# First feed-forward rows read before the last scan, later ones a tile at a time, and the sample's rows three blocks later

## The chip, the cores and the metric

The kernel runs on one core of a Trainium2 chip. The metric is the device time of one execution in microseconds (us). The engines are TensorE (PE in the profile; PEld is its weight load), VectorE (DVE), ScalarE (ACT), GpSimd (POOL) and SyncE (SP, which only issues DMAs here). Each engine works through its own queue in order; semaphores tie the queues together.

## What is computed

One layer of a streaming encoder, for a prompt of 2048 rows and a sample of 32 rows that continues from caches, all in float32 with 1024 channels:

```python
xn = rms_norm(x, norm_mix_g);  proj = xn @ w_in              # 1024 -> 2176 columns
y_a = conv_module(u_a)       # GLU, causal depthwise conv of width 31, layer norm, swish
y_b = rwkv7_mixer(u_b)       # delta-rule state update, 4 heads of 64: a scan over the rows
y_c = pool_mixer(u_c)        # trailing means over 2, 4, 8, 16 rows
y_d = window_attention(u_d)  # 4 query heads, 2 kv heads, window 128
x = x + concat(y_a, y_b, y_c, y_d) @ w_out
hn = rms_norm(x, norm_ffn_g)
x = x + (silu(hn @ w_gate) * (hn @ w_up)) @ w_down           # inner width 2816
```

The outputs are both streams' rows and the new states and caches.

## The kernel before

**Matrix products.** A float32 factor is split into a high part and a remainder (`fp32r`), and each product is three matmuls (lines 93 to 95 in helper `mm3`).

**Mixer stage.** The prompt goes through in `NB` = 8 blocks of 256 rows. For each block a string of letters gives the order in which its steps are issued: A is the projection of the other mixers, R the scan, n and N the norm of the next block's rows, B and S the next block's projection and the preparation of its scan, O the output projection of the block before, P and D the attention's preparation and the attention itself, L the pooling, C the convolution, Y the end of the scan's mixer. The last block has a string of its own, `ORDS`. Within the program, Tile's scheduler then sets each engine's order by issue order and by priorities (`high_priority(offset=...)`; R and Y have 1000). The attention of a block is two row tiles of 128, one after the other on single buffers: transposes `atp`, scores `asp`, softmax in `apr` on VectorE and ScalarE, transposes `aptp`, product `aot`, result `yhd` and `yld`.

**The sample.** Its 32 rows ride along with one block, `SB`: the block's projections are 288 rather than 256 columns wide, and its P, C and L follow there. R and O of the sample come one block later. `SB` is 1, the second block. Blocks one and two also read the raw weights and split them on ScalarE and on GpSimd or VectorE (`wraw`, `whl`); later blocks reload split copies from memory (`wk_i`, `wk_o`).

**Feed-forward, first half.** The 2080 rows are taken in three blocks `FB` of 704, 704 and 672 rows. For each, `ffn_x` reads six row tiles of `x2d`, norms them (`xs`, L1220) and transposes them into `xT` (TensorE `xps` L1224, evacuated by VectorE at L1226). It then forms the sums of a seven-product (Strassen-like) scheme in `ft` (L1234 to L1237). `ffn_ops` splits the seven operands into `xh` (ScalarE, L1251) and `xl` (VectorE, L1252). Then 11 pairs of column tiles follow; each pair is two halves, gate and up, of seven products of 12 matmuls `gu`. In a half VectorE also forms sums of weights (`wf`, L1265 to L1268) and evacuates `u` and `act` (L1299 to L1334), ScalarE makes `wh` and GpSimd `wl` (L1274, L1275).

```python
1212         for c in range(0, n, 128):                       # ffn_x, six row tiles
1219             rsqrt(st[:m, 1:2], st[:m, 0:1], 1.0 / D, RMS_EPS)
1220             V.tensor_scalar(xs[:m], xs[:m], st[:m, 1:2], None, op0=MUL)
...
1344     with tc.high_priority(offset=1500):
1345         xT = ffn_x(*FB[0], bank0)                        # behind the eighth block's steps
1346     xo = ffn_ops(xT, FB[0][1] // 2)
1347     out_proj(*pend)                                      # output projection of block eight
...
1358         for g in range(NP):
1359             if g == NP - 2 and i + 1 < len(FB):          # all six tiles of the next block
1360                 with tc.high_priority(offset=FNP):
1361                     xT = ffn_x(*FB[i + 1], ...)
1362             ffn_pair(r0, n, g, xo, H)
```

So before, the first block's rows are read and transposed after the last scan is issued, and a later block's six tiles and its sums are issued in one go late in the block ahead of it.

**Feed-forward, second half.** The inner activations go through memory (`act_d`) and are multiplied by the split down weights (`dn`, L1372 to L1408).

**Buffers.** The mixers' SBUF pools `b1`, `b2`, `b4` and `bv` lie on one side and are released together (`p0.close()`); the pool `fx` with `xT`, `xs` and `ft` is opened after that. `xT`, `ft` and each operand have one buffer.

Of the kernel before, what the change touches and what calls it, by code (L numbers as in the profile page):

```python
# [32 lines left out]
def layer(tc, ins, outs):  # L33
# [14 lines left out]
    SB = 1 if NB > 1 else 0  # L48
# [20 lines left out]
    ORDS = "ARnNBSOPLCYD,ARPDCLOY".split(",")  # L69
# [8 lines left out]
    SEP = 0  # L78
# [76 lines left out]
    b4 = p0.enter_context(tc.tile_pool(name="b4", bufs=1, side="right"))  # L155
    bv = p0.enter_context(tc.tile_pool(name="bv", bufs=1, side="right"))
# [12 lines left out]

    gmix = cp.tile([128, D], F32, tag="gm", name="gmix")  # L170
# [234 lines left out]
    def rs(sg, res):  # L405
        return res_s if sg is seg_s else res["p"]
# [4 lines left out]
    def sgs(b, o):  # L411
        return [sg for sg in (seg_p, seg_s) if at_block(sg, b, o)]
# [672 lines left out]
    def mix_y(outs_, ys):  # L1085
        for sg, o in outs_:
            rwkv_out(sg, *o, *yy(sg, ys)["b"])
# [63 lines left out]
    with tc.high_priority(offset=100000):  # L1151
        xhl = norm(0, norm_load(0))
    with tc.high_priority(offset=PB0):
        res = proj_b(0, *xhl)
        for sg in sgs(0, "R") if SEP else [seg_p]:
            rwkv_prep(sg, rs(sg, res))
    pend = None
    for b in range(NB):
        ys = y_tiles()
        cur = res  # L1160
        for o in ORDS[max(b - NB, -len(ORDS))]:
          with tc.high_priority(offset=OFF[o]) if o in OFF else ExitStack():
            if o == "R":
                ro = mix_b(b, cur, ys)
            if o == "Y":
                mix_y(ro, ys)
            if o == "O" and pend is not None:
                out_proj(*pend)
            if o == "A":
                proj(b, cur, *xhl)  # L1170
            if o == "P":
                mix_p(b, cur)
            if o == "D":
                mix_d(b, cur, ys)
            if o == "C":
                mix_a(b, cur, ys)
            if o == "L":
                mix_c(b, cur, ys)
            if o == "n" and b + 1 < NB:
                xn = norm_load(b + 1)  # L1180
            if o == "N" and b + 1 < NB:
                xhl = norm(b + 1, xn)
            if o == "B" and b + 1 < NB:
                res = proj_b(b + 1, *xhl)
            if o == "S" and b + 1 < NB:
                for sg in sgs(b + 1, "R") if SEP else [seg_p]:
                    rwkv_prep(sg, rs(sg, res))
        pend = (b, ys)
    p0.close()

# [13 lines left out]
    fx = pool2("x", "right", px2)  # L1204
    fo = pool2("o", "right")
# [3 lines left out]
    def ffn_x(r0, n, bank):  # L1209

        xT = fx.tile([128, 2 * NF * 128], F32, tag="xT", name="xT")[:, :KT * 2 * HM].rearrange("p (k t) -> p k t", k=KT)
        for c in range(0, n, 128):
            m = min(128, n - c)
            xs = fx.tile([128, D], F32, tag="xs", name="xs", bufs=XSB)
            st = fx.tile([128, 4], F32, tag="xst", name="xst", bufs=2)
            junk = fx.tile([128, D], BF16, tag="fjunk", name="fjunk")
            nc.sync.dma_start(xs[:m], x2d[r0 + c:r0 + c + m])
            S.activation(junk[:m], xs[:m], AF.Square, accum_out=st[:m, 0:1])
            rsqrt(st[:m, 1:2], st[:m, 0:1], 1.0 / D, RMS_EPS)
            V.tensor_scalar(xs[:m], xs[:m], st[:m, 1:2], None, op0=MUL)  # L1220
            for g in range(0, KT, 4):
                ps = bank()
                for j in range(4):
                    TE.transpose(ps[:, j, :m], xs[:m, (g + j) * 128:(g + j + 1) * 128], ident[:m, :m])  # L1224
                with tc.high_priority(offset=EVP):
                    V.tensor_tensor(xT[:, g:g + 4, c:c + m], ps[:, :, :m],  # L1226
                                    gcol[:, g:g + 4].unsqueeze(2).to_broadcast([128, 4, m]), op=MUL)
# [152 lines left out]
    for hf in range(D // 512):  # L1380
# [3 lines left out]
        for t in range(TT // 128 + 1):  # L1384
            n = min(128, TT - t * 128)
            e = t % 2
            af = d2.tile([128, NF, 128], F32, tag="af", name="af") if e else fx.tile(
# [9 lines left out]
            xr = d2.tile([128, 512], F32, tag="xr", name="xr", bufs=2)  # L1397
# [52 lines left out]
```

## Time and profile before

| | |
|---|---|
| median of 3 runs (range) | 2536.8 us (2535.28 to 2550.27) |
| profiled execution, and its span | 2535.49 us, 2533.8 us |
| mean granted TensorE clock | 0.975 |
| PE, DVE, ACT, POOL busy | 2401.4, 1729.2, 982.2, 977.3 us |
| instructions | 44039 |

The span runs from the first to the last instruction on the core. Busy time of PE is the union of overlapping matmuls, so it hides lost issue slots; the number of matmul records in a stretch tells more. A row "us, PE busy (x)" of the table of stretches gives its length, each engine's busy time and in brackets its instructions, then the granted clock and the DMA share. In the timeline a row is start, duration, engine, line, output<-input, and in square brackets how long the engine had waited and for whom.

### The profile page before, as it was taken

What the parts mean: (1) busy time and instruction counts of PE and PEld (TensorE: products, weight loads), DVE (VectorE), ACT (ScalarE), POOL (GpSimd) and SP (SyncE); (2) the same over time, 40 slices, a digit from 0 to 9 for tenths busy, and PEclk for the clock granted to TensorE, in tenths of its full rate; (3) what the DMA queues carried; (4) which work ended last, traced back from release to release, by engine and by line L of the source; (5) the groups of instructions that cost most, each with busy time, mean ns of one, the idle gap of its engine ahead of it and who ended that gap; (6) DMA issues with size and microseconds to landing.
All of it is one profiled execution on the core that took longest, in us unless ns stands there. A gap on an engine that the chain in (4) does not pass through costs nothing. (4 is left out here: it accounts for less than half of the span.)

```text
span 2533.8 us, 44039 instructions
## 1 busy us (share of the span) xinstructions
PE 2401.4 (95%) x16433; PEld 2196.0 (87%) x16433; DVE 1729.2 (68%) x3697; ACT 982.2 (39%) x2138; POOL 977.3 (39%) x834
## 2 busy tenths in 40 slices
PE   7789899999999999789999999998999899999999
PEld 6778788888988988689999999998999878878887
DVE  6798969896969698686877868678777432233221
ACT  5445453534353434434445443454444331122110
POOL 5543521211111112377677776676777310001000
PEclk9899899999999999899999999999999899999999
DMA  6556558566767676633433333334333465445441
GB/s 204 192 208 241 204 205 319 206 226 229 277 256 272 228 266 226 239 93 104 130 103 106 102 103 108 103 98 133 112 103 116 126 198 139 133 122 166 135 137 34
DMA packets 350747, 424.69 MB, mean 168 GB/s; under 512 B 24530, under 2 KB 300259, under 8 KB 326979
## 3 DMA queue, kind: packets, MB, share of 16 engines
q1 hardware_dynamic: 325304, 380.76, 46.4%
q10 hardware_dynamic: 25227, 41.10, 4.3%
q8 instruction: 129, 2.11, 0.3%
q14 instruction: 87, 0.71, 0.1%
HBM read 354.72 MB, written 67.18 MB: 167 GB/s over the span
## 5 line engine op out<-in xcount | busy, mean ns | idle before, releaser
L1275 POOL TENSOR_TENSOR wl<-wf,wh 128x512 fp32r<-128x512 f32 x462 | 661.8, 1438 | 241.0 <-PE gu L95 192.7
L93 PE MATMUL gu<-xh,wh 128*128 128x352 f32 (+1 forms) x1848 | 591.4, 324 | 25.8 <-DVE u L1302 19.2
L95 PE MATMUL gu<-xh,wl 128*128 128x352 f32 (+1 forms) x1848 | 598.6, 324 | 4.1 <-POOL wl L1275 4.1
L94 PE MATMUL gu<-xl,wh 128*128 128x352 f32 (+1 forms) x1848 | 597.6, 324 | 3.3 <-DVE xl L1252 3.2
L1274 ACT ACTIVATE wh<-wf 128x512 fp32r<-128x512 f32 x462 | 288.2, 630 | 434.2 <-PE gu L94 305.1
L93 PEld LDWEIGHTS gu<-xh,wh 128*128 128x128 f32 x1848 | 350.3, 190 | 31.1 <-DVE u L1302 19.0
L94 PEld LDWEIGHTS gu<-xl,wh 128*128 128x128 f32 x1848 | 351.6, 190 | 5.4 <-DVE xl L1252 5.4
L95 PEld LDWEIGHTS gu<-xh,wl 128*128 128x128 f32 x1848 | 351.0, 190 | 5.4 <-POOL wl L1275 5.3
L93 PE MATMUL dn<-dw,ah 128*128 128x512 f32 x704 | 277.4, 396 | 9.1 <-ACT dw L1376 6.7
L94 PE MATMUL dn<-dw,ah 128*128 128x512 f32 x704 | 276.0, 393 | 2.0 <-DVE dw L1377 1.9
L95 PE MATMUL dn<-dw,ah 128*128 128x512 f32 x704 | 275.6, 392 | 1.0 <-DVE ah L1396 1.0
L93 PE MATMUL pj<-xh,whl 128*128 128x256 f32 (+1 forms) x832 | 249.1, 302 | 11.8 <-ACT gb_s L526 3.1
L94 PE MATMUL pj<-xl,whl 128*128 128x256 f32 (+1 forms) x832 | 245.4, 297 | 0.7 <-DVE xl L144 0.6
L95 PE MATMUL pj<-xh,whl 128*128 128x256 f32 (+1 forms) x832 | 242.2, 295 | 3.9 <-POOL whl L387 3.9
L1395 ACT ACTIVATE ah<-af 128x1408 fp32r<-128x1408 f32 (+1 forms) x68 | 86.5, 1321 | 369.5 <-issue 291.8
L1408 DVE TENSOR_TENSOR xr<-xr,dn 128x512 f32<-128x512 f32 x32 | 22.0, 687 | 303.2 <-PE dn L95 303.2
L568 DVE SCALAR_TENSOR_TENSOR accp<-gbp,d_cws,accp 128x256 f32<-128x256 f32 x480 | 227.3, 501 | 0.8
L93 PEld LDWEIGHTS pj<-xh,whl 128*128 128x128 f32 x832 | 164.3, 198 | 23.5 <-issue 6.9
L95 PEld LDWEIGHTS pj<-xh,whl 128*128 128x128 f32 x832 | 162.0, 196 | 7.7 <-POOL whl L387 5.7
L94 PEld LDWEIGHTS pj<-xl,whl 128*128 128x128 f32 x832 | 164.0, 198 | 3.8 <-DVE xl L144 1.6
L93 PEld LDWEIGHTS dn<-dw,ah 128*128 128x128 f32 x704 | 133.0, 189 | 39.3 <-ACT dw L1376 7.4
L94 PEld LDWEIGHTS dn<-dw,ah 128*128 128x128 f32 x704 | 133.0, 189 | 31.5 <-DVE dw L1377 2.8
(512 smaller groups left out, 4764.0 us busy)
## 6 DMA issues: line engine op xcount, KB each, us to landing
whl<-wk_i SPq DMA_DIRECT2D x104, 1024.0 KB
whl<-wk_o SPq DMA_DIRECT2D x56, 1024.0 KB
af<-act_d SPq DMA_DIRECT2D x32, 1408.0 KB
wf<-in_ffn_w_gate_dram SPq DMA_DIRECT2D x132, 256.0 KB
wf<-in_ffn_w_up_dram SPq DMA_DIRECT2D x132, 256.0 KB
wk_i<-whl SPq DMA_DIRECT2D x16, 1024.0 KB
act_d<-act ACTq DMA_DIRECT2D x44, 352.0 KB
wraw<-in_w_in_dram SPq DMA_DIRECT2D x96, 128.0 KB
```

The lines of the kernel that those rows point to most:

```text
L93: TE.matmul(out, ah, bh, start=first, stop=False, skip_group_check=more)
L94: TE.matmul(out, ah, bl, start=False, stop=False, skip_group_check=more)
L95: TE.matmul(out, al, bh, start=False, stop=last, skip_group_check=more)
L568: V.scalar_tensor_tensor(acc[:, c, :], gb[:, c, j:j + T], cws[c][:, j:j + 1], acc[:, c, :], op0=MUL, op1=ADD)
L1274: S.activation(hi, q[nm], AF.Copy)
L1275: G.tensor_tensor(lo, q[nm], hi.bitcast(F32), op=SUB)
L1395: S.activation(ah[:, fs_, :n], af[:, fs_, :n], AF.Copy)
L1408: V.tensor_tensor(xr, xr, ps, op=ADD)
```

## The change

Four edits, in one diff:

- 14 products of the identity with itself, into a PSUM tile that nobody reads, first in TensorE's queue.
- `SB` is 4: the sample's rows go with the fifth block, its R and O with the sixth.
- `ffn_x` becomes a generator that yields after each row tile, and the sums become a function of their own, `ffn_sums`. A new letter X in the last block's string, behind P and ahead of R, runs `ffn_x` for the first block. D now stands behind R there. For that, `b1` is released alone at X, the other mixer pools lie on the other side, and PSUM for `xps` comes from the buffers `at` and `nx` rather than `at` and `rk`.
- Later blocks: one row tile in each of the pairs g = 2 to 7, the sums at g = 8.

```diff
-    SB = 1 if NB > 1 else 0
+    SB = 4 if NB > 5 else 0
-    ORDS = "ARnNBSOPLCYD,ARPDCLOY".split(",")
+    ORDS = "ARnNBSOPLCYD,APXRDCLOY".split(",")
-    p0 = ExitStack()
+    p0, pb = ExitStack(), ExitStack()
-    b1 = p0.enter_context(tc.tile_pool(name="b1", bufs=1, side="right"))
-    b2 = p0.enter_context(tc.tile_pool(name="b2", bufs=2, side="right"))
+    b1 = pb.enter_context(tc.tile_pool(name="b1", bufs=1, side="right"))
+    b2 = p0.enter_context(tc.tile_pool(name="b2", bufs=2, side="left"))
...
+    with tc.high_priority(offset=200000):
+        warm = px([128, 128], "warm", "rk")
+        for _ in range(14):
+            TE.matmul(warm, ident, ident, start=True, stop=True)
...
     def ffn_x(r0, n, bank):
...
+            yield xT
+
+    def ffn_sums(xT, n):
+
         H = n // 2
         q = {"b11": xT[:, 0:4, 0:H], ...}
-        ft = fx.tile([128, 3, 4, HM], F32, tag="ft", name="ft")
+        ft = fq.tile([128, 3, 4, HM], F32, tag="ft", name="ft")
...
-        return px([128, 4, 128], "xps", ("at", "rk")[banks[0] % 2])
-
-    with tc.high_priority(offset=1500):
-        xT = ffn_x(*FB[0], bank0)
-    xo = ffn_ops(xT, FB[0][1] // 2)
+        return px([128, 4, 128], "xps", ("at", "nx")[banks[0] % 2])
...
+            if o == "X":
+                pb.close()
+                fx = pool2("x", "right", px2)
+                for xT in ffn_x(*FB[0], bank0):
+                    pass
...
+    fq, fo = pool2("q", "right", px2), pool2("o", "right")
+    xo = ffn_ops(ffn_sums(xT, FB[0][1]), FB[0][1] // 2)
     out_proj(*pend)
...
         if i:
             with tc.high_priority(offset=FNP):
-                xo = ffn_ops(xT, H)
+                xo = ffn_ops(q, H)
         for g in range(NP):
-            if g == NP - 2 and i + 1 < len(FB):
+            if g == NP - 9 and i + 1 < len(FB):
+                rows = ffn_x(*FB[i + 1], lambda: pnr.tile([128, 4, 128], F32, tag="nr", name="xps"))
+            if g >= NP - 9 and i + 1 < len(FB):
                 with tc.high_priority(offset=FNP):
-                    xT = ffn_x(*FB[i + 1], lambda: pnr.tile([128, 4, 128], F32, tag="nr", name="xps"))
+                    xT = next(rows, xT)
+                    if g == NP - 3:
+                        q = ffn_sums(xT, FB[i + 1][1])
             ffn_pair(r0, n, g, xo, H)
```

The rest of the diff moves the main loop behind these definitions and takes two tiles of the second half (`af`, `xr`) from other pools.

The first place is TensorE's queue at the end of the last scan. `yp` are the scan's last products, `fp` its final state, `atp`, `asp`, `aptp`, `aot` the steps of one attention tile, `po` the output projection. Before, the first tile's `aot` already stands between the scan's last rows:

```order
L922 MATMUL yp<-vtokp,krp 64x64 x4
L922 MATMUL yp<-wwp,trp 64x64 x4
L724 MATMUL aot<-apt,avt 64x256
L1027 MATMUL fp<-ident,stp_238 128x128 x2
L724 MATMUL aot<-apt,avt 64x256 x3
L662 MATMUL atp<-ident,aqn 128x128 x2
L663 MATMUL atp<-ident,aqn 128x128
L95 MATMUL po<-whl,ylb 128x256
```

After the change, seven `po` rows follow the scan, and then this (`yt` are the transposes of the scan's result, `xps` those of the first feed-forward rows, `lna` and `lnb` belong to the convolution's layer norm):

```order
L1046 MATMUL yt<-ident,gynp 128x128 x4
L1186 MATMUL xps<-ident,xs 128x128 x8
L1186 MATMUL xps<-ident,xs 128x64 x8
L666 MATMUL atp<-ident,aqn 128x128 x2
L667 MATMUL atp<-ident,aqn 128x128
L1062 MATMUL sto<-ident,carryp 7x128
L583 MATMUL lna<-ident,accp 128x128 x2
L685 MATMUL asp<-ktb,aqt 128x256 x4
L583 MATMUL lna<-ident,accp 128x128 x2
L593 MATMUL lnb<-ident,lnhp 128x128 x4
L723 MATMUL aptp<-ident,apr 128x128 x8
L728 MATMUL aot<-apt,avt 64x256 x4
```

What moved: the first block's transposes (28 of 44 stand still further up, among the scan's steps) came forward, and the whole attention of the first tile went behind the scan; the second tile's follows it.

The second place is VectorE's queue at the start of the second feed-forward block, right behind the last `xl` of its operands. Before:

```order
L1252 TENSOR_TENSOR xl<-xT,xh 128x704
L1266 TENSOR_TENSOR wf<-wf 128x512
L1267 TENSOR_TENSOR wf<-wf 128x512
L1334 TENSOR_TENSOR act<-act,u_17576 128x352
L1302 TENSOR_TENSOR u_17674<-u_17673,gu 128x352
L1268 TENSOR_TENSOR wf<-wf 128x512
L1305 TENSOR_TENSOR u_17674<-u_17674,gu 128x352
L1299 TENSOR_TENSOR u_17817<-u_17816,gu 128x352
```

After (L1188 evacuates transposes of the third block's rows into `xT`; 12 such rows, six scalings `xs` and the eight sums stand in this and the next seven halves):

```order
L1218 TENSOR_TENSOR xl<-xT,xh 128x704
L1232 TENSOR_TENSOR wf<-wf 128x512
L1233 TENSOR_TENSOR wf<-wf 128x512
L1300 TENSOR_TENSOR act<-act,u_17594 128x352
L1268 TENSOR_TENSOR u_17692<-u_17691,gu 128x352
L1188 TENSOR_TENSOR xT<-xps,gcol 128x4x128
L1234 TENSOR_TENSOR wf<-wf 128x512
L1271 TENSOR_TENSOR u_17692<-u_17692,gu 128x352
L1265 TENSOR_TENSOR u_17835<-u_17834,gu 128x352
L1188 TENSOR_TENSOR xT<-xps,gcol 128x4x128
```

What moved: the next block's rows now follow the operands' split at once, and no such rows are left in the later halves, where they stood before.

More of the change, by code (lines that the diff above doesn't have):

```diff
@@ L149, in layer @@
     b3 = p1.enter_context(tc.tile_pool(name="b3", bufs=2, side="left"))
[L150 removed]
+    p0, pb = ExitStack(), ExitStack()
     pmm = p1.enter_context(tc.tile_pool(name="pmm", bufs=3, space=PSUM, side="left"))
     ppx = p1.enter_context(tc.tile_pool(name="ppx", bufs=8 - 3, space=PSUM, side="right"))
[L153 to L156 removed]
+    b1 = pb.enter_context(tc.tile_pool(name="b1", bufs=1, side="right"))
+    b2 = p0.enter_context(tc.tile_pool(name="b2", bufs=2, side="left"))
+    b4 = p0.enter_context(tc.tile_pool(name="b4", bufs=1, side="left"))
+    bv = p0.enter_context(tc.tile_pool(name="bv", bufs=1, side="left"))
     PSB = {"nx": 1, "rk": 2, "at": 2}
@@ L1149, in out_proj @@
                     SD.dma_start(dst[:, cw], xr[:PT])
[L1151 to L1189, printed above, removed]
     TT, NP = SEQ + DS, NF // 2
@@ L1203, in layer @@
     px2 = ExitStack()
-    fx = pool2("x", "right", px2)
-    fo = pool2("o", "right")
     gcol = cp.tile([128, KT], F32, name="gcol")
@@ L1341, in bank0 @@
         banks[0] += 1
-        return px([128, 4, 128], "xps", ("at", "rk")[banks[0] % 2])
-    with tc.high_priority(offset=1500):
-        xT = ffn_x(*FB[0], bank0)
-    xo = ffn_ops(xT, FB[0][1] // 2)
+        return px([128, 4, 128], "xps", ("at", "nx")[banks[0] % 2])
+    with tc.high_priority(offset=100000):
+        xhl = norm(0, norm_load(0))
+    with tc.high_priority(offset=PB0):
+        res = proj_b(0, *xhl)
+        for sg in sgs(0, "R") if SEP else [seg_p]:
+            rwkv_prep(sg, rs(sg, res))
+    pend = None
+    for b in range(NB):
+        ys = y_tiles()
+        cur = res
+        for o in ORDS[max(b - NB, -len(ORDS))]:
+          with tc.high_priority(offset=OFF[o]) if o in OFF else ExitStack():
+            if o == "R":
+                ro = mix_b(b, cur, ys)
+            if o == "Y":
+                mix_y(ro, ys)
+            if o == "O" and pend is not None:
+                out_proj(*pend)
+            if o == "A":
+                proj(b, cur, *xhl)
+            if o == "P":
+                mix_p(b, cur)
+            if o == "X":
[3 more added lines that the diff above has]
+                    pass
+            if o == "D":
+                mix_d(b, cur, ys)
+            if o == "C":
+                mix_a(b, cur, ys)
+            if o == "L":
+                mix_c(b, cur, ys)
+            if o == "n" and b + 1 < NB:
+                xn = norm_load(b + 1)
+            if o == "N" and b + 1 < NB:
+                xhl = norm(b + 1, xn)
+            if o == "B" and b + 1 < NB:
+                res = proj_b(b + 1, *xhl)
+            if o == "S" and b + 1 < NB:
+                for sg in sgs(b + 1, "R") if SEP else [seg_p]:
+                    rwkv_prep(sg, rs(sg, res))
+        pend = (b, ys)
+    p0.close()
+    fq, fo = pool2("q", "right", px2), pool2("o", "right")
+    xo = ffn_ops(ffn_sums(xT, FB[0][1]), FB[0][1] // 2)
     out_proj(*pend)
@@ L1386, in layer @@
             e = t % 2
-            af = d2.tile([128, NF, 128], F32, tag="af", name="af") if e else fx.tile(
+            af = d2.tile([128, NF, 128], F32, tag="af", name="af") if e else fq.tile(
                 [128, 3 * 4 * HM], F32, tag="ft", name="af")[:, :NF * 128].rearrange("p (f t) -> p f t", f=NF)
@@ L1396, in layer @@
                 V.tensor_tensor(lo[:, fs_], af[:, fs_, :n], ah[:, fs_, :n].bitcast(F32), op=SUB)
-            xr = d2.tile([128, 512], F32, tag="xr", name="xr", bufs=2)
+            xr = fx.tile([128, D], F32, tag="xs", name="xr", bufs=XSB)[:, :512]
             nc.sync.dma_start(xr[:n], x2d[t * 128:t * 128 + n, w])
```

## The prediction

> **What bounds the kernel now.** First the page's busy times.
>
> ```profile
> PE 2401.4 (95%) x16433; PEld 2196.0 (87%) x16433; DVE 1729.2 (68%) x3697; ACT 982.2 (39%) x2138; POOL 977.3 (39%) x834
> ```
>
> TensorE bounds the kernel on average. Its busy time unites overlapping products, though, so 95% does not mean that only 5% can be won. I therefore read stretches next, and in them the count of records, since a starved TensorE issues fewer.
>
> ```profile
> core 0: us, PE busy (x) PEld busy (x) DVE busy (x) ACT busy (x) POOL busy (x), PEclk, DMA share, GB/s
> 475.00:565.00 90.00, 88.49 (x817) 79.37 (x816) 83.20 (x270) 37.60 (x105) 14.62 (x13) 1.00 0.65 236
> 565.00:663.00 98.00, 95.95 (x870) 86.96 (x869) 72.94 (x240) 47.80 (x133) 17.90 (x20) 1.00 0.67 238
> 663.00:792.00 129.00, 126.19 (x1187) 115.99 (x1187) 109.16 (x350) 49.06 (x133) 19.68 (x20) 1.00 0.73 260
> 1000.00:1060.00 60.00, 51.17 (x368) 45.09 (x366) 30.15 (x68) 24.02 (x57) 13.79 (x19) 0.89 0.78 278
> 1060.00:1120.00 60.00, 45.10 (x240) 40.92 (x241) 56.14 (x59) 29.85 (x52) 53.01 (x30) 0.89 0.32 94
> 1120.00:1220.00 100.00, 100.00 (x633) 99.90 (x633) 66.88 (x87) 42.99 (x77) 69.65 (x53) 1.00 0.36 111
> 1220.00:1280.00 60.00, 55.35 (x340) 53.72 (x339) 53.18 (x65) 24.39 (x47) 41.79 (x31) 0.97 0.38 113
> 1380.00:1430.00 50.00, 44.92 (x274) 43.41 (x273) 47.27 (x52) 25.97 (x45) 35.90 (x23) 1.00 0.30 94
> 1550.00:1600.00 50.00, 42.71 (x243) 41.76 (x243) 40.67 (x45) 15.67 (x29) 28.94 (x20) 0.90 0.24 72
> ```
>
> Two paces serve as yardsticks. In the mixer, 475 to 792 us holds 817 + 870 + 1187 = 2874 products in 317 us, 9.07 per us. In the feed-forward stage, 1120 to 1220 us holds 633 in 100 us, 6.33 per us. At that pace half a pair (84 products) takes 13.3 us, and VectorE, busy 66.88 of 100 us, has 4.4 us free in it.
>
> What the other stretches fall short of, divided by their pace, is what they lose:
>
> - 1000 to 1060 us: 544 would go through at the mixer's pace, 368 did, 19 us (a mixed stretch, so an upper bound); 1060 to 1120: 380 less 240, 22 us. This is the passage from the last scan to the feed-forward.
> - 1220 to 1280: 380 less 340, 6.3 us. Here the second block's rows are read, within the first block.
> - 1380 to 1430, the start of the second block: 316 less 274, 6.7 us.
> - 1550 to 1600: 316 less 243, 11.6 us; the third block's rows.
>
> So the change aims at about 66 us of lost slots. VectorE is the busiest beside TensorE in these starts (56.14 of 60, 53.18 of 60, 47.27 of 50 us): TensorE waits there for work that VectorE has yet to do.
>
> **Part 1, the first rows ahead of the last scan.** The timeline at the passage, TensorE's, ScalarE's and GpSimd's rows:
>
> ```profile
> 981.78 0.44 PE L662 MATMUL atp<-ident,aqn 128*128 128x128 f32 x2
> ...
> 1003.75 0.44 PE L916 MATMUL yp<-stp,arp 128*64 128x128 f32 x4
> 1006.69 0.44 PE L662 MATMUL atp<-ident,aqn 128*128 128x128 f32 x2
> 1009.58 0.38 PE L1042 MATMUL yt<-ident,gynp 128*128 128x128 f32 x2
> ...
> 1034.42 0.39 ACT L727 ACTIVATE yhd<-aot 128x256 fp32r<-128x256 f32 x1 [4.03 <-PE aot L724]
> 1060.71 0.43 PE L93 MATMUL gu<-xh,wh 128*128 128x352 f32 x1
> ...
> 1060.41 17.77 POOL L1275 TENSOR_TENSOR wl<-wf,wh 128x512 fp32r<-128x512 f32 x8 [1.82 <-ACT wh L1274]
> ```
>
> Let T be 1003.75 us, the scan's last product. Before, one attention tile (981.78 to 1006.69, 25 us) ran beside the scan, the other (1006.69 to 1034.42, 28 us) behind it. The first `gu` started at T + 57, and another 22 us were then lost, so the stage started in effect at T + 79.
>
> Now both tiles stand behind the scan. The scan's `yt` stay at T + 6 and 16 of the 44 row transposes follow (2 us at 0.12 each, the spacing shown in part 4): T + 8. Both durations above had other work between their steps. The chain of a tile by itself I take as 14 us, half the longer row; its ends are 14 and 28, and I lean to the short one since little else is left for VectorE there. The first tile has the convolution's layer norm beside it, for which I add 3 us: 17. The second has 57 output products queued between its rows, 7 us at 0.12, so 21: T + 46. Then 107 output products wait in order behind the last `aot`, 13 us: `gu` at T + 59, 2 us *later* than before. The gain lies in what is left for VectorE then:
>
> ```profile
> L1220 DVE TENSOR_SCALAR xs<-xs,xst 128x1024 f32<-128x1024 f32 x15 | 17.4, 1161 | 3.6 <-POOL xst L118 3.2
> L1226 DVE TENSOR_TENSOR xT<-xps,gcol 128x512 f32<-128x512 f32 x30 | 20.3, 682 | 7.8 <-PE xps L1224 7.8
> L1235 DVE TENSOR_TENSOR ft<-xT,ft 128x704 f32<-128x704 f32 x4 | 4.6, 1152 | 0.0
> L1252 DVE TENSOR_TENSOR xl<-xT,xh 128x704 fp32r<-128x704 f32 x16 | 21.8, 1387 | 0.0
> ```
>
> The rows are normed and evacuated already. Six sums at 1.15 and 14 splits at 1.3 us remain, 25 us, and 3 us of evacuations of the attention: 28 us, begun at T + 46, so 15 are left at T + 59, against some 24 before. If 24 cost 22 us, 15 cost 14: an effective start at T + 73, **-6 us**. Bounds: at best the second tile's chain hides behind 3 us of its products, so `gu` starts at T + 56, and half of the 14 are lost, T + 63, -16; with 28 us per tile and the products inside it, T + 8 + 56 + 13 = T + 77, effective T + 91, +12. The 28 transposes among the scan's steps cost TensorE 28 x 0.12 = 3.4 us ahead of T, the first tile's products moved behind T give about that back; I set them against each other. GpSimd's eight `wl` took 17.77 us, 2.2 each, one for each 1.9 us of `gu` at full pace or less: they start with the pair before as after, so I cost them at nothing; if the earlier `xl` no longer hide them, they add no more than the +12.
>
> **Part 2, later rows one tile a pair.** A block's rows cost VectorE 6 scalings at 1.16, 12 evacuations at 0.68 and 8 sums at 1.15 us: 7 + 8 + 9 = 24 us. By the changed queue order they stand at the start of the block, spread over 7 halves in block one and 8 in block two. Block one has 7 x 4.4 = 31 us free for 24, so I leave 3 us of the 6.3 lost. Block two must also do its own 14 splits first, 14 x 1.3 = 18: 42 us against 8 x 4.4 = 35, so 7 us lost in place of 6.7 + 11.6 = 18.3. That is 3 - 6.3 + 7 - 18.3 = -14.6 us if VectorE's free time were smooth. One half carries five of the moved instructions at once, so I take about two thirds: **-9 us**. Bounds: 0 (the same work at another place) and -18 (all but 7 of the 25 recovered). The transposes cost TensorE the same as before.
>
> **Part 3, the sample in the fifth block.** The first blocks, where it was, and the fourth:
>
> ```profile
> 164.00:306.00 142.00, 128.70 (x1095) 113.89 (x1095) 129.08 (x378) 64.92 (x191) 56.75 (x70) 0.93 0.61 220
> 306.00:396.00 90.00, 84.75 (x741) 74.60 (x741) 67.12 (x230) 48.50 (x152) 25.76 (x32) 0.93 0.59 209
> 396.00:475.00 79.00, 77.39 (x685) 70.96 (x685) 73.98 (x244) 24.97 (x68) 12.67 (x15) 1.00 0.74 278
> ```
>
> 164 to 396 us holds 1836 products in 232 us, 202 at the yardstick: 30 us lost. But the first of these stretches also splits raw weights (GpSimd 56.75 us against 19.68 in 663 to 792, ScalarE 64.92 against 49.06). The waits on TensorE that name the sample there are short; this is the longest:
>
> ```profile
> 201.16 0.40 PE L93 MATMUL pj<-xh,whl 128*128 128x288 f32 x1 [3.08 <-ACT gb_s L526]
> ```
>
> The work only moves, from a stretch with VectorE at 129.08 of 142 us to ones with 72.94 of 98 and 109.16 of 129. I take **0**, with bounds -20 (two thirds of the 30) and +40 (the 25 of the rival below, and 15 more, half of what the early blocks lose now, if the fifth block loses too); this is the change's most open term.
>
> **Part 4, identity products first.**
>
> ```profile
> 1.13 0.29 POOL masks.py:199 TENSOR_SCALAR_AFFINE_SELECT ident<-ident 128x128 f32<-128x128 f32 x1
> ...
> 12.09 3.67 PE L140 MATMUL xps<-ident,xt 128*128 128x128 f32 x16 [12.09 <-DVE xt L133]
> 18.10 0.41 PE L94 MATMUL pj<-xl,whl 128*128 128x256 f32 x1
> 18.31 0.41 PE L95 MATMUL pj<-xh,whl 128*128 128x256 f32 x1
> ...
> 21.33 0.28 PE L93 MATMUL pj<-xh,whl 128*128 128x256 f32 x1
> 21.45 0.28 PE L94 MATMUL pj<-xl,whl 128*128 128x256 f32 x1
> ...
> 80.02 0.58 PE L95 MATMUL pj<-xh,whl 128*128 128x256 f32 x1 [3.91 <-POOL whl L387]
> ```
>
> The same product starts every 0.21 us at 18 us and every 0.12 us at 21.3 us: TensorE works at near half pace for its first 9 us. The first real products wait for `xt` until 12.09 us whatever stands ahead. Fourteen products at 0.23 us, the 0.21 above a little rounded up, are 3.2 us; the identity is made at 1.42 us, so they end near 5, in idle time, and 7 idle us follow before 12.09. After an idle time of only 3.91 us, at 80.02, the granted clock was low again:
>
> ```profile
> 80.00:84.00 4.00, 3.98 (x18) 3.99 (x19) 3.93 (x7) 0.83 (x2) 3.75 (x5) 0.50 0.44 127
> ```
>
> So 7 idle us should undo what the products bring: **0**. If they did leave TensorE fast, the 25 product slots of 0.21 us from the end of the transposes (15.8) to 21 us would be 0.09 shorter each, -2, and the transposes with them, -4 at most.
> On this the Trainium skill, page "TensorE: Matmul & The Clock Gate", section "What's actually happening", states that the array runs at half clock by default and after one idle window of about 3.4 us, and at full clock after one busy window of that length. By it the 14 products could lift the clock, and the idle time would drop it again: 0, as the row at 80 says; without the drop the sum would be 4 us lower. The trace differs from it in the rise, which took about 9 us from the first transpose here.
>
> The other edits (PSUM for `xps` from `nx` rather than `rk`, `af` and `xr` from other pools, pools on other sides) change no instruction. `nx` holds the norm transposes of a next block, which the last block does not have, so nothing contends for it. I cost them at nothing; if a reuse did wait, it is in the +12 of part 1.
>
> **The sum**, on the profiled execution: 2535.5 - 6 - 9 + 0 + 0 = 2520.5. The median shown is 1.3 us above that execution, so 2522 us. Its own range is 2508 to 2535.
>
> **The rivals.**
>
> *Faster still.* The sample's rows, not the raw weights, hold up the early blocks. For it speaks VectorE's 129.08 of 142 us where the sample's wider steps stand; against it GpSimd's and ScalarE's splitting in the same stretch, and TensorE's short waits for sample tiles. Two thirds of 30 recovered: 2502.
>
> *The other side: VectorE becomes the bound in the sixth block.* The sample's scan and output now fall into 663 to 792 us, where VectorE has 20 us free. At a share of 0.94 (396 to 475, 73.98 of 79) TensorE was not starved; above it I expect it to be. At the pace of 164 to 306 us (1095 in 142, 7.71 per us) the 1187 products take 154 us rather than 129: +25, 2547 us. It decides where the moved work passes about 12 us (121 of 129). Against it: the sample has 32 rows where a block has 256.
>
> *Slow attention.* Each tile takes 28 us even with VectorE free: +12 rather than -6, so 2540.
>
> *The rows don't do what they should.* They land at a block's start, just where `xl` of the same block is wanted, and part 2 gives 0: 2531.
>
> **How the numbers follow.** Forecast 0.37, faster still 0.25, sixth block 0.17, slow attention 0.13, rows at the start 0.08. The range must reach most of the first three: 2495 (the 2502 with part 2 near its own bound) to 2550. This kernel's three runs spread by 0.6%, so 1% (25 us) is about what can be told from no change. Under 2511 lie the faster rival and a tenth of the forecast: 0.29. Above 2562 lies only a sixth block worse than the price above, or two bad cases together: 0.09. The rest, 0.62, is within 1%.
>
> **What would show it.** Part 1: the first `gu` 55 to 62 us behind the last `yp`, `po` rows waiting for `aptp` or `aot` of the second tile, and more than 300 products in the 60 us from the first `gu`. It is wrong if `gu` comes past T + 70 or before T + 45. Part 2: no 50 us inside blocks one and two with fewer than 280 products, and the shortfall gathered in the blocks' first 100 us. Part 3: the pace of the second and third mixer blocks within 3% of before with the sample gone; the sixth block near 9 products per us. Part 4: the first real products still at 12 us, 0.21 apart until about 21. The whole would be wrong if the scans' own steps change pace in blocks that the diff does not name, since no term covers that.

## The result, and the profile after

The changed kernel took 2562.14 us (median of 5 runs, 2555.77 to 2563.5) against 2537.02 us (5 runs, 2535.28 to 2550.27). The ratio is 1.0067, 95% interval 1.0046 to 1.0088: slower by some 17 us, where 15 us faster was forecast. (The two medians lie 25 us apart, but these five runs of before are few; in the later comparisons the kernel before has medians of 2542 to 2544 us over 17 to 26 runs. All sizes below go by the ratio, each to the runs of before that were timed beside it.)

The profiled execution took 2555.77 us, its span is 2554.1 us, 20.3 us more than before. First the stretches of the changed kernel: the passage to the feed-forward stage and its first two blocks whole. The fence behind it has the end of the passage and the same two blocks of before; the columns are those of the table of stretches.

```profile
core 0: us, PE busy (x) PEld busy (x) DVE busy (x) ACT busy (x) POOL busy (x), PEclk, DMA share, GB/s
1020.00:1070.00 50.00, 32.19 (x196) 24.40 (x196) 23.20 (x55) 23.48 (x63) 12.98 (x17) 0.73 0.38 123
1070.00:1101.00 31.00, 19.55 (x112) 18.64 (x112) 22.74 (x33) 10.43 (x16) 0.00 (x0) 0.72 0.56 189
1101.46:1418.70 317.24, 306.11 (x1895) 302.38 (x1894) 235.67 (x275) 141.01 (x252) 237.04 (x168) 0.99 0.36 109
1418.70:1732.30 313.60, 303.80 (x1894) 300.19 (x1893) 236.70 (x286) 135.52 (x242) 222.38 (x157) 1.00 0.35 107
```

```profile
1034.80:1060.70 25.90, 21.36 (x161) 20.65 (x159) 13.79 (x27) 8.33 (x15) 2.48 (x5) 0.87 0.79 295
1060.71:1392.56 331.85, 311.37 (x1897) 305.08 (x1896) 255.87 (x301) 149.59 (x266) 246.63 (x170) 0.97 0.36 107
1392.56:1713.30 320.74, 307.77 (x1900) 304.85 (x1899) 240.92 (x287) 135.32 (x242) 221.77 (x157) 0.98 0.34 103
```

The two feed-forward blocks got *shorter*, by 14.6 and 7.1 us. The time is lost ahead of them: between the last scan product (1020.2) and the first `gu` (1101.5), 81 us, TensorE is busy little more than 60% of the time, at a granted clock of 0.73.

The same account can be made for every run of this study. The columns are the time of the last `yp`, the time from there to the first `gu`, blocks one and two of the feed-forward (1848 `gu` each), and the rest of the span, all from the timeline of the profiled executions; the ratio is that of the timed runs. (In stretches that an edit leaves alone the columns still differ by several us: with the sample in the second block the last `yp` of the kernels in the table lies between 1004.4 and 1008.6, and with the feed-forward's later rows as before, block two takes 318 to 326 us in all the kernels of this study. The profile of before was also one of its shorter ones. So sizes are taken from the ratio and places from the columns.)

| kernel | last `yp` | to first `gu` | block one | block two | rest | ratio to before (95%) |
|---|---|---|---|---|---|---|
| before | 1004.4 | 56.3 | 331.9 | 320.7 | 820.5 | 1 |
| changed | 1020.2 | 81.3 | 317.2 | 313.6 | 821.8 | 1.0067 (1.0046 to 1.0088) |
| e1 rows | 1007.1 | 56.4 | 329.5 | 313.1 | 823.2 | 0.9957 (0.9941 to 0.9973) |
| e2 sample | 1026.0 | 52.4 | 332.7 | 321.3 | 823.3 | 1.0052 (1.0036 to 1.0068) |
| e3 first rows | 1005.0 | 84.5 | 312.1 | 321.6 | 823.5 | 1.0018 (1.0004 to 1.0032) |
| e4 identity | 1008.2 | 54.3 | 331.8 | 320.5 | 824.5 | 1.0005 (0.9986 to 1.0024) |
| e5 one quarter | 1008.4 | 78.8 | 314.8 | 325.1 | 823.8 | 1.0014 (0.9999 to 1.0030) |
| e6 attention ahead | 1008.6 | 92.9 | 310.4 | 325.8 | 823.1 | 1.0079 (1.0063 to 1.0095) |
| e8 changed, sample second | 1008.1 | 82.2 | 316.7 | 314.1 | 822.1 | 1.0037 (1.0021 to 1.0053) |
| e9 rows spread | 1005.1 | 55.6 | 327.8 | 316.5 | 822.5 | 0.9950 (0.9935 to 0.9966) |

So 15.8 us of the profile's 20.3 are lost in the mixer, 25.0 in the passage, and 21.7 come back in the two blocks. The passage, TensorE's timeline of the changed kernel:

```profile
1020.17 0.40 PE L926 MATMUL yp<-wwp,trp 64*64 64x64 f32 x8
...
1028.55 1.97 PE L1186 MATMUL xps<-ident,xs 128*128 128x128 f32 x8 [4.61 <-DVE xst L117]
...
1032.38 0.69 PE L666 MATMUL atp<-ident,aqn 128*128 128x128 f32 x2
...
1044.34 1.11 PE L593 MATMUL lnb<-ident,lnhp 128*128 128x128 f32 x4 [7.15 <-ACT lnhp L589]
...
1050.27 0.69 PE L666 MATMUL atp<-ident,aqn 128*128 128x128 f32 x2
...
1068.63 1.08 PE L728 MATMUL aot<-apt,avt 128*64 128x256 f32 x8 [0.26 <-ACT apt L724]
...
1074.79 0.55 PE L93 MATMUL po<-whl,yha 128*128 128x256 f32 x1 [3.83 <-DMA whl<-wk_o]
1083.43 0.58 PE L93 MATMUL po<-whl,yhc 128*128 128x256 f32 x1 [4.04 <-DMA whl<-wk_o]
...
1093.76 0.39 PE L93 MATMUL po<-whl,yhc 128*128 128x256 f32 x1 [2.63 <-DMA whl<-wk_o]
...
1101.46 0.41 PE L93 MATMUL gu<-xh,wh 128*128 128x352 f32 x1
```

The attention tiles run one after the other as forecast, 18 us (1032.4 to 1050.3) and 19 us (to 1069.7). What was not forecast is behind them: from the last `aot` on, the last output products (107 in the forecast, 108 in this trace) need 31 us, not 13. Three waits for the split output weights make up 10.5 of these 31 us; for the rest the slow pace of the stretch (clock 0.72) is a reading, not a test.

### The profile page after: what moved, and what is told of

It reads as the page before. It is cut to its first block, busy times and chain, and to the rows that moved or that the text cites. A ratio compares the mean times of both kernels' runs of the same rounds, so it can differ in the third digit from the quotient of the medians.

```text
span 2554.1 us, 44102 instructions
## 1 busy us (share of the span) xinstructions
PE 2406.2 (94%) x16461; PEld 2196.5 (86%) x16461; DVE 1725.9 (68%) x3697; ACT 982.6 (38%) x2138; POOL 969.7 (38%) x834
```

## The experiments

### Each part alone (e1 to e4)

The theory read from the trace after the change: each part acts by itself; the rows gain, the sample and the first rows lose, the identity does nothing.

**e1, later rows one tile a pair, nothing else.** `ffn_x` as the generator, `ffn_sums` apart, and

```diff
-            if g == NP - 2 and i + 1 < len(FB):
+            if g >= NP - 9 and i + 1 < len(FB):
                 with tc.high_priority(offset=FNP):
-                    xT = ffn_x(*FB[i + 1], ...)
+                    xT = next(rows, xT)
+                    if g == NP - 3:
+                        q = ffn_sums(xT, FB[i + 1][1])
```

> The kernel before with one part of the change: later rows one tile a pair (g = 2 to 7, sums at g = 8). Theory M (each part acts by itself, the sizes read from the trace after the change): the first gu to the last gu took 948 us before and 926 us after, so this part alone gives -15 to -22 us, 2515 to 2522. Rival C (the feed-forward stage only looks shorter because its start came later and found more work done ahead of it): 0, 2533 to 2541.

Measured 0.9957 (0.9941 to 0.9973), 11 us faster, so rival C (no gain) falls. The part works alone, less than the trace after the change seemed to say. The blocks:

```profile
1063.56:1393.10 329.54, 311.31 (x1903) 304.39 (x1901) 257.58 (x301) 150.28 (x266) 247.55 (x170) 0.98 0.35 108
1393.10:1706.20 313.10, 303.78 (x1894) 300.18 (x1893) 236.53 (x287) 135.53 (x242) 222.20 (x157) 1.00 0.34 106
```

Block one gains 2.4 us, which is within what executions differ by, and block two 7.6. The first quarter of block one takes *longer* (104.1 us against 96.1). (The expectations call such a stretch a pair. It is 462 of the 1848 `gu`, a quarter of a block; a pair is 168, 26.9 us at full pace.) By real pairs, the first three take 112.7 us rather than 103.0, and the fifth to seventh, where the second block's rows stood before, 80.7 rather than 93.3. So the rows cost time at their new place too, next to the splits of the first block's operands, but less than at the old one.

**e2, the sample in the fifth block, nothing else.**

```diff
-    SB = 1 if NB > 1 else 0
+    SB = 4 if NB > 5 else 0
```

> The kernel before with SB = 4 and nothing else. Theory M: of the mixer's products the same count stands 15 us earlier at 450 us and 18 us later at 811 us in the trace after, so the early blocks gain 15 and the later ones lose some 30: +12 to +18 us, 2549 to 2555. Rival X (the loss late in the mixer comes from the feed-forward's rows read there): the early gain stays, -15 us, 2522.

Measured 1.0052 (1.0036 to 1.0068), 13 us slower, as theory M had it; rival X falls, since no feed-forward row is read there. Nearly the same numbers of TensorE's products in four stretches of the mixer, before and then e2:

```profile
16.00:190.00 174.00, 150.54 (x1216) 135.37 (x1216) 139.02 (x399) 84.55 (x248) 88.32 (x108) 0.90 0.60 205
190.00:494.00 304.00, 286.28 (x2446) 254.89 (x2446) 261.07 (x839) 137.87 (x405) 86.71 (x110) 0.96 0.65 235
494.00:762.00 268.00, 262.15 (x2418) 238.91 (x2418) 220.07 (x692) 116.78 (x324) 48.94 (x49) 1.00 0.68 245
762.00:1004.00 242.00, 235.07 (x2177) 214.65 (x2175) 206.95 (x661) 94.24 (x258) 35.55 (x35) 0.99 0.69 250
```

```profile
16.00:183.00 167.00, 145.29 (x1210) 131.51 (x1211) 132.52 (x359) 81.33 (x231) 89.83 (x111) 0.92 0.67 229
183.00:489.00 306.00, 281.56 (x2452) 250.57 (x2451) 257.28 (x780) 138.83 (x390) 83.41 (x94) 0.96 0.66 235
489.00:775.00 286.00, 273.09 (x2411) 247.37 (x2410) 225.25 (x754) 120.12 (x356) 53.67 (x58) 0.98 0.65 230
775.00:1026.00 251.00, 244.26 (x2218) 219.52 (x2220) 213.17 (x702) 93.47 (x261) 39.81 (x43) 1.00 0.65 235
```

The first stretch gains 7 us, the second gains nothing although the sample left it, the third loses 18 and the fourth 9. VectorE is no fuller in the third (225 of 286 us, 0.79, against 220 of 268, 0.82). TensorE's idle time there rises from 5.9 to 12.9 us, and its busy time by 11 us.

**e3, the first rows ahead of the scan, nothing else.** Letter X with its pools and PSUM. P and X now stand ahead of R; D stands behind R, as it did before:

```diff
-    ORDS = "ARnNBSOPLCYD,ARPDCLOY".split(",")
+    ORDS = "ARnNBSOPLCYD,APXRDCLOY".split(",")
```

> The kernel before with the first feed-forward rows ahead of the last scan and the attention behind it (with the pools that this needs); sample in the second block, later rows in one go, no identity products. Theory M: first gu 81 us behind the last yp rather than 57, +24, less 4 that come back in the first pairs: +18 to +24 us, 2555 to 2561. Rival X: also 10 us or more late in the mixer: +28 to +36, 2565 to 2573. The prediction had -6.

Measured 1.0018 (1.0004 to 1.0032), 5 us slower and not 18. The first `gu` came 84.5 us behind the last `yp`, but block one then took 312.1 us rather than 331.9, so theory M had the place right and what comes back too small. Rival X falls: the last `yp` is where it was. Of the 19.8 us that come back in block one, 14.7 lie in its first three pairs (88.3 us rather than 103.0), and the rest in the fifth to seventh (88.1 rather than 93.3).

**e4, the identity products alone**: the four lines of the diff.

> The kernel before with the 14 identity products first in TensorE's queue. Theory M: nothing, 2533 to 2541, the first real products still 0.21 us apart until about 21 us. Rival W: the products cost something in the first block (300 to 600 mixer products stood 3 to 6 us later in the trace after): +3 to +9 us, 2540 to 2546.

Measured 1.0005 (0.9986 to 1.0024): no difference that can be told. W's larger values fall; a cost of 3 to 6 us lies within the interval. The timeline and the stretches of e4:

```profile
1.47 5.41 PE L173 MATMUL warm<-ident 128*128 128x128 f32 x28 [1.47 <-POOL ident masks.py:199]
12.65 3.57 PE L140 MATMUL xps<-ident,xt 128*128 128x128 f32 x16 [5.77 <-DVE xt L133]
...
18.40 0.28 PE L94 MATMUL pj<-xl,whl 128*128 128x256 f32 x1
18.52 0.28 PE L95 MATMUL pj<-xh,whl 128*128 128x256 f32 x1
...
8.00:12.00 4.00, 0.00 (x0) 0.00 (x0) 1.70 (x9) 1.44 (x5) 1.61 (x4) 0.64 0.32 51
12.00:16.00 4.00, 3.35 (x16) 3.17 (x16) 3.38 (x4) 2.76 (x7) 3.50 (x5) 0.50 0.38 111
16.00:20.00 4.00, 3.66 (x29) 3.30 (x28) 1.72 (x3) 1.52 (x5) 1.11 (x2) 1.00 0.79 248
```

At 18.4 us the products stand 0.12 us apart; in the trace of before they stood 0.21 apart until about 21 us. That is no mark of the identity products, though. e2, which has none, does the same:

```profile
12.10 3.67 PE L140 MATMUL xps<-ident,xt 128*128 128x128 f32 x16 [12.10 <-DVE xt L133]
...
17.10 0.28 PE L95 MATMUL pj<-xh,whl 128*128 128x256 f32 x1
17.22 0.28 PE L93 MATMUL pj<-xh,whl 128*128 128x256 f32 x1
```

Of the 14 kernels without the identity products, 8 reach the full pace 8.2 to 9.6 us behind the first real product (before 9.0), and 6 after 4.8 to 6.1 us (e2 5.0); the three with them take 4.5 to 5.5 us (e4 4.5). So it isn't shown that the products bring the rise forward. What e4 does show agrees with the forecast: the granted clock dropped in the idle time (0.64, then 0.50), and the first 16 transposes took 3.57 us, against 3.67 before. At the 600th mixer product e4 is no further than before (113 us against 107).

### What holds up the passage (e5, e6)

**e5, the loads of the output weights taken away.** Six of the eight loads of the last output projection are left out, on top of e3:

```diff
-            wt = load_unit(f"o{q}", dma, 256)
+            if not one or q == 0:
+                wt = load_unit(f"o{q}", dma, 256)
...
-    out_proj(*pend)
+    out_proj(*pend, one=True)
```

> The kernel of the run with the first rows alone ahead of the scan, but the last output projection reads the split weights of its first quarter only and multiplies by them in all four (so six of its eight loads are left out, and its output columns are others). Theory L (the 107 products behind the attention wait for these loads, in three buffers that the attention holds): the waits of 4.0, 3.9 and 2.4 us go, the products between the last aot and the first gu take 13 to 17 us rather than 30, first gu 66 to 71 us behind the last yp rather than 84.5; ratio about 0.994 against the first rows alone, so 0.994 to 0.998 against before. Rival K (TensorE's low clock and the evacuations hold these products up): first gu still 80 us or more behind, ratio to before 1.000 to 1.003.

Measured 1.0014 (0.9999 to 1.0030), against 1.0018 for e3. From the last `aot` to the last `po` it took 18.3 us rather than 30.4, and no wait for `whl` is left. That is the direction of theory L, though not its 13 to 17 us, and 84 products stand there rather than 108, since more ran earlier. Another wait took the place of the loads:

```profile
1073.99 0.58 PE L93 MATMUL po<-whl,yha 128*128 128x256 f32 x1 [4.12 <-DVE xr L1149]
```

That is the evacuation of the products before. The first `gu` came 78.8 us behind the scan, not 66 to 71, and in the end no time that can be measured was won; the ratio is the one that rival K gave. The loads do hold the output products up; they are not, by themselves, what the first rows cost.

**e6, attention in front of X**, again on e3:

```diff
-APXRDCLOY
+APDXRCLOY
```

> The first rows alone ahead of the scan, but D in front of X, so that the attention has the scan's idle places first (string APDXRCLOY rather than APXRDCLOY). Theory L: the attention ends as before some 30 us behind the last yp, first gu 54 to 60 us behind it, ratio to before 0.997 to 1.001; the rows come late as before, so the first pair of gu takes about 96 us again. Rival: X ahead of the scan costs the tail time wherever D stands, first gu over 75 us behind.

Measured 1.0079 (1.0063 to 1.0095), 20 us slower; the first `gu` came 92.9 us behind the last `yp`. Theory L's forecast for this run is wrong, the rival's right. The last attention product started already 17.7 us behind the scan, 12 us earlier than before, but then the convolution, which is issued behind X, is late. In TensorE's queue 40 of the rows' 48 transposes stand between the last `aot` and the convolution's first products `lna`, and they wait for VectorE's scalings `xs`:

```profile
1035.10 1.97 PE L1182 MATMUL xps<-ident,xs 128*128 128x128 f32 x8 [5.18 <-DVE xs L1178]
...
1043.29 1.94 PE L1182 MATMUL xps<-ident,xs 128*128 128x128 f32 x8 [4.24 <-DVE xs L1178]
...
1049.22 0.69 PE L579 MATMUL lna<-ident,accp 128*128 128x128 f32 x2 [1.54 <-DVE sto L1060]
...
1059.93 1.12 PE L589 MATMUL lnb<-ident,lnhp 128*128 128x128 f32 x4 [6.42 <-ACT lnhp L585]
1064.05 0.58 PE L93 MATMUL po<-whl,yha 128*128 128x256 f32 x1 [3.01 <-ACT yha L549]
```

The last block's output products all stand behind one that waits for the convolution's result `yha` until T + 55 (T the last `yp`, 1008.6). So it is not the attention's place as such. In both orders that were run, what stands behind the rows becomes the late input of the output projection: the attention in e3, the convolution here.

### Do the parts add up (e8)

The changed kernel with `SB = 1`.

> The changed kernel with the sample back in the second block (SB = 1), the other three parts kept. Theory A (the parts add up: -0.43% rows, +0.18% first rows, +0.05% identity): ratio 0.998, within 0.996 to 1.000. Rival I (the parts hinder each other, since the four alone add up to +0.32% and the whole change measured +0.67%): 1.001 or more.

Measured 1.0037 (1.0021 to 1.0053), as rival I had it. The parts do not add up: alone they sum to -0.43 + 0.18 + 0.05 = -0.20%, so 0.57%, some 14 us, come in by their standing together (by an estimate from the four intervals, 0.2 to 0.9%). The table places about half of it. With the first rows read early, block one takes 312.1 us (e3); adding the spread of the later rows makes it 316.7, a loss of 4.6, where the spread alone gained 2.4. Block two gains as much as it did alone (7.5 and 7.6). By pairs of block one:

| | before | e1 rows | e3 first rows | e8 both |
|---|---|---|---|---|
| pairs 1 to 3, us | 103.0 | 112.7 | 88.3 | 99.9 |
| pairs 5 to 7, us | 93.3 | 80.7 | 88.1 | 80.7 |

Part 1 takes work away from VectorE in the first pairs, part 2 puts the second block's rows there, and that costs some 10 to 12 us with or without part 1. What part 2 wins in pairs 5 to 7 is 12.6 us alone, but only 7.4 behind part 1, since e3 had already lost less there. Where the other half of the 14 us lies isn't shown, and e8 holds the identity products too, whose share wasn't taken apart.

### Rows without the raised priority (e9)

```diff
-                with tc.high_priority(offset=FNP):
-                    xT = next(rows, xT)
-                    if g == NP - 3:
-                        q = ffn_sums(xT, FB[i + 1][1])
+                xT = next(rows, xT)
+                if g == NP - 3:
+                    q = ffn_sums(xT, FB[i + 1][1])
```

> Later rows one tile a pair as in the change, but issued without the raised priority, so that VectorE's queue has one scaling and two evacuations to a half nearly to the block's end instead of up to five such rows in the block's first halves. Theory P (what the rows gain is given back in the first pairs, where they meet the operands' splits: pair one 104.1 us against 96.1, the first pair of block two 88.3 against 79.1): these pairs return to 94 to 98 and 78 to 82 us, the others keep 74 to 76, ratio to before 0.990 to 0.993. Rival Q (the first pairs are long because of the rows' loads and scalings as such, wherever they stand): the time only moves to later pairs, ratio 0.995 to 0.997 as with the raised priority.

Measured 0.9950 (0.9935 to 0.9966), the fastest version of the study, though not to be told from e1. The first quarters of the two blocks return to 97.1 and 84.0 us, as P has it (the second a little above its range), but the third quarters, in which the last evacuations and the eight sums now stand, take 78.9 and 80.2 us rather than 73.9. So mostly Q: the 24 us of VectorE work cost some TensorE time wherever they are put.

### The sample's place (e7, e10, e11, e12)

The kernel before with one number changed, `SB`.

> The kernel before with SB = 2, the sample in the third block. Theory S (only the first two blocks, which split raw weights, leave TensorE places in which the sample is hidden; in any later block it costs its full time): ratio 1.003 to 1.006, as with the fifth block (1.0052). Rival V (the sixth block's VectorE share decides for the fifth): the third block's own stretches, VectorE 0.94 and 0.92 of the time, are fuller than the fifth's and sixth's (0.74, 0.85), so at least 1.007, or, if the fifth block has another fault, 1.000.

> The kernel before with SB = 3. The third block measured 1.0121 and the fifth 1.0052, the second is 1. Theory S (raw weights' idle places hide the sample, a fixed cost elsewhere) would give one value for all three and has failed on the third; theory H (the cost is that of the holes in the scan stretches that the sample's work leaves or fills, so it depends on the blocks that it meets): a value of its own between 1.003 and 1.012. Rival E (blocks of even number are bad, odd ones good): 0.998 to 1.002.

> The kernel before with SB = 0. Theory H: no gain, 1.000 to 1.010, since the first block's own preparation already waits for loads and splits and the sample's wider projection comes ahead of the first scan. Rival S (early idle places hide the sample): 0.996 to 1.000.

> The kernel before with SB = 6; the sample's scan and output then go with the last block. Theory H: 1.003 to 1.015, since the last block's scan has no next block's projection beside it and the sample's output joins the products ahead of the feed-forward. Rival G (the sample's work fills the last scan's idle places): 0.995 to 1.000.

| the sample's block | first | second | third | fourth | fifth | seventh |
|---|---|---|---|---|---|---|
| ratio | 1.0048 | 1 | 1.0121 | 1.0085 | 1.0052 | 1.0118 |
| interval | 1.0030 to 1.0065 | | 1.0101 to 1.0140 | 1.0063 to 1.0108 | 1.0036 to 1.0068 | 1.0098 to 1.0138 |
| last `yp`, us | 1024.6 | 1004.4 | 1038.1 | 1031.1 | 1026.0 | 1055.4 |

Every other place that was tried costs 0.5 to 1.2% (the sixth and the last weren't). Theory S (early idle places hide the sample) falls with the first and the third block, E (even and odd) and G fall too. V's forecast for the third block came true, but not its rule. The stretches that it took for the third block's, 396 to 565 us, are the fourth's, where that sample's scan goes (in the timeline of before the third block's scan lies at 356 to 382 us). By VectorE's share in the block that takes the scan the order of costs is wrong: 0.74 (the fifth) goes with 1.0085, 0.85 (the sixth) with 1.0052. The three values for which theory H gave a range lie in it; the ranges were wide, so that supports it little.

### Which of the sample's steps (e13, e14, e15)

The digits are the blocks by which the sample's R, P, C, L and O follow its projection. e13 and e14 keep the sample in the second block, e15 has it in the fifth:

```diff
-    DLY = dict(zip("RPCLO", (int(x) for x in "10001")))
+    DLY = dict(zip("RPCLO", (int(x) for x in "40004")))   # e13
+    DLY = dict(zip("RPCLO", (int(x) for x in "40334")))   # e14
+    DLY = dict(zip("RPCLO", (int(x) for x in "00000")))   # e15, with SB = 4
```

> The kernel before, the sample in the second block, but its scan (R) and output projection (O) only with the sixth block, as in the change. Theory R (the sample's scan is a chain that used to stand beside the third block's scan and now lengthens the sixth's): ratio 1.003 to 1.008, like the whole move (1.0052). Rival J (the wider projection, attention, convolution and pooling in the fifth block are the cost): 0.998 to 1.002.

> As the run with the scan and output late, and the sample's convolution and pooling in the fifth block as well; projection and attention stay in the second. Theory R: within 0.002 of the run with the scan and output late. Rival J: the two steps bring at least half of the 0.52%, 0.003 or more above that run.

> The sample in the fifth block (SB = 4) with scan and output in the fifth block too rather than the sixth. Theory R: the chain only lengthens another scan, so 1.003 to 1.010. Rival J: 1.003 to 1.007 as before, as the scan's place doesn't matter. Rival D (the sixth block is the cause, by its VectorE): 0.996 to 1.002.

Measured 1.0014 (0.9999 to 1.0030), 1.0018 (1.0004 to 1.0033) and 1.0060 (1.0037 to 1.0083). Moving the scan and the output to the sixth block costs a quarter of the whole move by the middle value, and perhaps nothing; moving convolution and pooling too adds nothing that can be told. With the scan in the fifth block the cost is the same as in the sixth. So R falls, D falls, and what is left of J is narrower than it said: by the middle values about 0.34% of the 0.52% goes with the sample's projection and attention in the fifth block. That is a difference of two ratios, so it assumes that the steps add up; no run moves these two alone, and which of them it is wasn't told apart. The timeline of e2 shows only short waits for the sample's attention:

```profile
730.72 0.73 PE L681 MATMUL asp<-kt_s,aqt 64*32 64x160 f32 x8 [0.57 <-DVE kt_s L675]
...
748.70 0.88 PE L719 MATMUL aptp<-ident,apr 32*128 32x32 f32 x3 [1.52 <-ACT apr L701]
```

Nor is it shown why the second block is the cheapest place. One trace suggests, and no run proves, that it is a matter of which stretch is left without a partner. In e2, where the sample's scan used to follow, the two engines take turns: from 440 to 470 us TensorE is full and VectorE busy 11.5 of 30 us, then TensorE waits and VectorE is full. In the same 49 us of before, at not quite the same work, both are busy most of the time. The fence has e2's two stretches and then before's.

```profile
440.00:470.00 30.00, 30.00 (x255) 27.05 (x254) 11.52 (x31) 16.31 (x45) 6.73 (x7) 1.00 0.49 167
470.00:489.00 19.00, 13.95 (x124) 11.73 (x123) 18.31 (x57) 8.01 (x23) 5.54 (x6) 0.73 0.39 133
440.00:470.00 30.00, 29.43 (x280) 26.02 (x281) 26.32 (x89) 12.98 (x36) 7.54 (x10) 1.00 0.62 226
470.00:489.00 19.00, 18.48 (x166) 16.43 (x164) 16.52 (x71) 7.53 (x23) 0.11 (x1) 1.00 0.57 197
```

## Why the prediction was wrong, point by point

**Sign and range.** 2522 us and a range of 2495 to 2550 stood against 2562. The chance of 0.62 for within 1% is where the result fell by its ratio, on the slower side. From -15 us to +17 us are 32 us. By the middle values part 1 accounts for 11 of them, part 3 for 13, and some 9 come from the parts standing together, for which the sum had no term; parts 2 and 4 nearly cancel (-2 and +1).

**Part 1, forecast -6, measured alone +0.18% (5 us).** The step that failed is the 107 output products "x 0.12 = 13". They took 31 us in the changed kernel and 30.4 in e3. A better number was in the trace of before: from the end of the attention (1034.8) to the first `gu` (1060.7) it took 25.9 us for 161 records, some 120 of them output products, with the clock at 0.87. That would have been nearer, though still short of 31. A pitch measured at full speed was multiplied by a count in a stretch with 10.5 us of waits for loads and a clock of 0.72; with the loads taken away (e5), evacuations held the products up instead. The start of that chain was 4 us off as well (the row transposes wait 4.61 us for `xst`, so the attention began at T + 12, not T + 8), and 18 + 19 us for the tiles against 17 + 21 was right. The first `gu` at T + 81 instead of T + 59 is thereby explained. The other end of the sum was too low: -8 us in lost slots behind the start was forecast, and block one gave back 19.8 us in e3. VectorE entered it without any rows to evacuate, and 14.7 of the 19.8 lie in the first three pairs; why the fifth to seventh lost 5 us less isn't shown. Two mis-sizings, +25 and -12, hid each other in part. The rival "slow attention" gave a `gu` at T + 77, near by luck: its tiles did not take 28 us. Two readings were off without weight: the trace of the changed kernel holds 48 row transposes rather than 44 (32 of them ahead of the scan's end, not 28), and the scan's last product stands at 1004.4, not 1003.75.

**Part 2, forecast -9, measured alone -0.43% (11 us).** Right, and in block two by its mechanism (7.6 us); block one's 2.4 us can't be told from the spread of executions, and its first three pairs pay 10 us for the rows. The sign of at least 280 products in any 50 us failed: the changed kernel has 249 early in block one and 256 at the turn to block two. The condition that the sum lacked is the other part: with the first rows early, the spread has less to win in block one (e8 against e3).

**Part 3, forecast 0, measured alone +0.52% (13 us).** The step that failed is "the work only moves": it cost 13 us to move. The bounds of -20 and +40 held it, being wide. In e2 the early blocks gain 5 us and the later ones lose 27 by the profile; why the same work costs more there stays open. The rival had the sign, and its place was wrong: putting scan and output into the sixth block costs 0.14% (-0.01 to 0.30), and VectorE was not fuller. The clue for the faster rival, 30 us lost in the early blocks, was worth 5 us.

**Part 4, forecast 0, measured 0.05% (-0.14 to 0.24).** The number was right, and nothing here contradicts the reason: the clock dropped in the idle time, and the first 16 transposes ran at their old pace. The size of the products was off: the profile has 28 records for the 14 of them, 5.41 us rather than 3.2, and 5.77 us idle behind them. The sign named for this part, 0.21 us apart until about 21 us, was a bad one, since kernels without the products reach the full pace anywhere between 16.6 and 21.9 us.

**The whole.** Alone the parts sum to +0.32% and the whole is 0.67% (0.46 to 0.88). By itself this difference is no larger than the intervals of the five ratios taken together; that the parts hinder each other rests on e8, 0.37% against -0.20%.

## What to carry to other kernels

When a step is pushed past another, price what stands behind the last arrival by the row that shows that very stretch, loads and evacuations included, and not by count times pitch. Two edits that change the load of the same engine in the same stretch need not add up: measure them together before adding their gains. A piece of work that rides along with one round of a tuned pipeline can cost 0.5 to 1.2% merely by riding along with another, and neither VectorE's load there nor early or late told which. A change at the start of a program is judged against more than one trace of before, since the starts themselves differ.

## What was unexpected of the hardware

How long TensorE keeps half pace at the start differs between traces that have nothing ahead of the first real product: in 8 of 14 it lasted 8.2 to 9.6 us, in 6 of 14 only 4.8 to 6.1 us. Each kernel has one trace, so whether the kernel or the execution decides isn't known. The records show a granted clock of 1.00 from 12 to 20 us in before, where the products stand 0.21 us apart, as in e2, where they stand 0.12 apart from 17 us on (the first fence is before's, the second e2's):

```profile
12.00:16.00 4.00, 3.75 (x17) 3.24 (x17) 2.91 (x5) 2.77 (x7) 3.11 (x5) 1.00 0.49 141
16.00:20.00 4.00, 3.85 (x16) 3.56 (x17) 2.04 (x4) 2.04 (x5) 0.93 (x2) 1.00 0.70 227
```

```profile
16.00:20.00 4.00, 3.52 (x27) 3.33 (x28) 2.14 (x4) 2.15 (x6) 1.16 (x3) 1.00 0.70 227
```

So at the start of this program the pitch of the products tells more than the clock's row. By the Trainium skill, page "TensorE: Matmul & The Clock Gate", section "What's actually happening", one busy window of about 3.4 us brings the full clock. The shorter starts come within some 3 us of that; the longer ones don't agree with it.
